# Softmax gradient over 8192 rows: all transfers on one queue, blocks moved as even and odd partitions

## The chip, the cores and the metric

One core of a Trainium2 chip runs the kernel. The metric is the device time of one execution in microseconds (us); lower is better. Before the change it was 1248.48 us, the median of three runs (1247.92 to 1248.65).

A core has engines that run their own instruction streams: TensorE (PE, hardly used here), VectorE (DVE), ScalarE (ACT), GpSimd (POOL) and SyncE (SP, which only issues transfers). Sixteen DMA engines move data between the main memory (HBM) and the on-chip memory (SBUF, 128 partitions). A transfer is issued from an engine's stream: SP and ACT each have a queue of their own, and both queues are served by the same sixteen DMA engines. Engines wait for each other and for transfers by semaphores.

## The reference

The gradient of the cross entropy with respect to the logits: a softmax of every row, less one at the label's place.

```python
logits = np.random.randn(8, 1024, 8192).astype(np.float32)
labels = np.random.randint(0, 8192, (8, 1024)).astype(np.int32)
...
logits_max = np.max(logits, axis=-1, keepdims=True)
exp_logits = np.exp(logits - logits_max)
softmax = exp_logits / np.sum(exp_logits, axis=-1, keepdims=True)
one_hot[batch_idx, seq_idx, labels] = 1.0
return (softmax - one_hot).astype(np.float32)
```

That is 268.4 MB read and 268.4 MB written.

## The kernel before

**Tiling.** The 8192 rows of 8192 floats are cut into B = 32 blocks of 256 rows. Partition p of a block holds the two consecutive rows 2p and 2p+1 (G = 2), each 32 KB, so that a block is 8 MB and, on each partition, 64 KB that lie together in HBM and in SBUF. `X` has room for three blocks (SLOTS = 3); block b lives in slot b % 3, and is worked on in place. What the code calls row t is one of the two rows of every partition, 128 x 8192 floats or 4 MB; there are T = 64 of them, two to a block (t0 and t1).

**The work on one row t.** `row_max` (VectorE) takes the negated maximum of each partition's row. `exponentials` (ACT) writes exp(x - max) over the row, and adds up the sum on the way. `mark` (two ACT instructions) makes one byte for each column, 1 at the label, in a PSUM tile `hot` that has a place for two rows; it may only overwrite a place when `finish` of two rows before is done. `finish` (VectorE) takes the reciprocal of the sum and does exp x reciprocal - byte in one pass over the row. Then the row can be stored.

**Order of the work.** All engines' instructions come from one hand-written loop over blocks. ORDER is "r" for every block: VectorE's stream is max(t1), finish(t0), max(t0 of the next block), finish(t1), and so on. The maximum of the next block's first row is taken, and its exponential issued, before this block is finished, and a row is stored as soon as it is finished.

**Transfers.** Each block's loads and stores have a kind, by the letter in LOADS and STORES, which selects pieces from PIECES: "r" is one row t at a time (128 partitions, runs of 32 KB); "s" is one row as even and as odd partitions (64 partitions, 32 KB); "w" is the whole block (128 partitions, 64 KB). Before, the first three blocks are loaded as "s", the even halves on SP's queue (`nc.sync`) and the odd ones on ACT's (`nc.scalar`); two blocks follow as "r", then 24 as "w" and the last three as "r", all on SP. All stores are "r", on ACT's queue, behind a wait for `finish`. The very last two rows are stored as two halves of columns each (`sides`), the first row on SP and the second on ACT. A load into a slot waits for the stores of the block that was there. `run` adds the waits and the semaphore's increment to an instruction; every instruction of the profile therefore has the line in `run` at which it is issued (L76 before the change).

Of the kernel before, what the change touches and what calls it, by code (L numbers as in the profile page):

```python
# [7 lines left out]
P = 128  # L8
G = 2
SLOTS = 3  # L10

LOADS = "sssrrwwwwwwwwwwwwwwwwwwwwwwwwrrr"
STORES = "rrrrrrrrrrrrrrrrrrrrrrrrrrrrrrrr"
ORDER = "rrrrrrrrrrrrrrrrrrrrrrrrrrrrrrrr"


@with_exitstack
def kernel(
# [6 lines left out]
    nc = tc.nc  # L25
# [11 lines left out]
    T = N // P  # L37
    B = T // G
# [3 lines left out]
    o_b = o_nv.rearrange("(b p j) v -> b p j v", p=P, j=G)  # L42
# [4 lines left out]
    X = const.tile([P, SLOTS, G, V], fp32)  # L47
# [11 lines left out]
    m, s, r = (const.tile([P, T], fp32, name=n) for n in ("m", "s", "r"))  # L59
# [4 lines left out]
    with tc.tile_critical():  # L64
        sem = tc.alloc_semaphore
        got = [[sem(f"got{i}{q}") for q in range(4)] for i in range(SLOTS)]
        put = [[sem(f"put{i}{q}") for q in range(4)] for i in range(SLOTS)]
# [3 lines left out]
        def run(engine, waits, counter, method, **operands):  # L71

            waits = list(dict.fromkeys(waits))
            for w in waits[:-1]:
                engine.wait_ge(*w)  # L75
            instruction = getattr(engine, method)(**operands)  # L76
            for w in waits[-1:]:
                instruction._wait_ge(*w)
            step = 16 if method == "dma_start" else 1
            instruction.then_inc(counter, step)  # L80
            count[counter.name] = count.get(counter.name, 0) + step
            return counter, count[counter.name]

        every, rows = slice(0, P), slice(0, G)
        one = [slice(j, j + 1) for j in range(G)]
        halves = [slice(i, P, 2) for i in range(2)]
        sides = [slice(i * V // 2, (i + 1) * V // 2) for i in range(2)]
        PIECES = {
            "r": [(every, js) for js in one],
            "s": [(ps, js) for js in one for ps in halves],  # L90
            "w": [(every, rows)],
        }

        def meets(a, b):
# [3 lines left out]
        loaded, stored, sides_done = {}, {}, {}  # L98
        maxed, summed, marked, finished, freed = {}, {}, {}, {}, {}

        def load(b):
            loaded[b] = []
            before = stored.get(b - SLOTS, [])
            for q, piece in enumerate(PIECES[LOADS[b]]):
                ps, js = piece
                free = [w for other, w in before if meets(piece, other)]
                queue = nc.scalar if LOADS[b] == "s" and ps == halves[1] else nc.sync
                w = run(
                    queue, free, got[b % SLOTS][q], "dma_start",
                    out=X[ps, b % SLOTS, js, :], in_=x_b[b, ps, js, :],  # L110
                )
                loaded[b].append((piece, w))

        def store(t):
            b, j = divmod(t, G)
            stored.setdefault(b, [])
            if t >= T - G:
                for i, cs in enumerate(sides):
                    w = run(
                        nc.sync if t == T - G else nc.scalar, [sides_done[t][i]], put[b % SLOTS][G * j + i],  # L120
                        "dma_start", out=o_b[b, every, one[j], cs], in_=X[every, b % SLOTS, one[j], cs],
                    )
                    stored[b].append(((every, one[j]), w))
                return
            for q, piece in enumerate(PIECES[STORES[b]]):
                ps, js = piece
                if js.stop != j + 1:
                    continue
                w = run(
                    nc.scalar, [finished[t]], put[b % SLOTS][q], "dma_start",  # L130
                    out=o_b[b, ps, js, :], in_=X[ps, b % SLOTS, js, :],
                )
                stored[b].append((piece, w))

        def row(t):
            return X[:, t // G % SLOTS, t % G, :]
# [4 lines left out]
        def row_max(t):  # L141
            b, j = divmod(t, G)
            arrived = {w[0].name: w for piece, w in loaded[b] if meets(piece, (every, one[j]))}
            maxed[t] = run(
                nc.vector, arrived.values(), dve, "tensor_reduce",
                out=m[:, t : t + 1], in_=row(t), axis=mybir.AxisListType.X, op=Alu.max, negate=True,
            )

        def exponentials(t):
            w = run(  # L150
                nc.scalar, [maxed[t]], act, "activation",
                out=row(t), in_=row(t), func=Act.Exp, bias=m[:, t : t + 1], scale=1.0,
                accum_out=s[:, t : t + 1],
            )
            summed[t] = w

        def mark(t):
            if t >= T:
                return
            w = run(  # L160
                nc.scalar, ([made] if t < G else [freed[t - G]]) + ([marked[t - 1]] if t else []), act, "activation",
                out=away[:], in_=count16[:], func=Act.Abs, bias=at(word, t), scale=1.0,
            )
            marked[t] = run(
                nc.scalar, [w], act, "activation",
                out=hot[:, t % G, :], in_=away[:], func=Act.Relu, bias=at(unit, t), scale=at(minus, t),
            )

        def finish(t):
            w = run(nc.vector, [summed[t]], dve, "reciprocal", out=r[:, t : t + 1], in_=s[:, t : t + 1])  # L170
            bytes_ = hot[:, t % G, :].bitcast(u8)
            sides_done[t] = []
            for i, c in enumerate(sides if t >= T - G else [slice(0, V)]):
                last = run(
                    nc.vector, [marked[t], w] if i == 0 else [], dve, "scalar_tensor_tensor",
                    out=row(t)[:, c], in0=row(t)[:, c], scalar=r[:, t : t + 1], in1=bytes_[:, c],
                    op0=Alu.mult, op1=Alu.subtract,
                )
                sides_done[t].append(last)
            finished[t] = freed[t] = last  # L180

        w_raw = run(nc.scalar, [], lab_got, "dma_start", out=lab_raw[:], in_=lab_bp)
        for b in range(SLOTS):
            load(b)
        w = run(nc.gpsimd, [], pool, "memset", ap=ident[:], constant=0.0)
        w_ident = run(
            nc.gpsimd, [w], pool, "affine_select",
            out=ident[:], in_=ident[:], compare_op=Alu.not_equal, fill=1.0,
# [8 lines left out]
        for j in range(G):  # L197
            w = run(
                nc.tensor, [w_ident, w_lab], pe, "transpose",
                out=lab_ps[:, j, :], in_=lab_f[:, j, :], identity=ident[:],  # L200
            )
        w = run(nc.vector, [w], dve, "tensor_copy", out=lab[:], in_=lab_ps)
        w = run(
            nc.vector, [w], dve, "tensor_scalar",
            out=part[:], in0=lab[:], scalar1=2, scalar2=None, op0=Alu.arith_shift_right,
        )
        w_word = run(
            nc.vector, [w], dve, "tensor_scalar",
            out=word[:], in0=part[:], scalar1=-1.0, scalar2=None, op0=Alu.mult,
        )  # L210
        w = run(
            nc.vector, [w_word], dve, "tensor_scalar",
            out=lab[:], in0=lab[:], scalar1=3, scalar2=None, op0=Alu.bitwise_and,
        )
        w = run(
            nc.vector, [w], dve, "tensor_copy", out=minus[:], in_=lab[:]
        )
# [3 lines left out]
            out=unit[:], in0=minus[:], scalar1=0.0, scalar2=powers[0], op0=Alu.is_equal, op1=Alu.mult,  # L221
# [21 lines left out]
        mark(1)  # L243
        for b in range(B):
            t0, t1 = b * G, b * G + 1
            nxt = t1 + 1
            if ORDER[b] == "b":
                if t0 not in maxed:
                    row_max(t0)
                    exponentials(t0)  # L250
                row_max(t1)
                exponentials(t1)
                finish(t0)
                store(t0)
                mark(t0 + G)
                finish(t1)
                store(t1)
                mark(t1 + G)
                if b + SLOTS < B:
                    load(b + SLOTS)  # L260
                continue
            if t0 not in maxed:
                row_max(t0)
                exponentials(t0)
            row_max(t1)
            finish(t0)
            exponentials(t1)
            store(t0)
            mark(t0 + G)
            ahead = nxt < T and ORDER[b + 1] == "r"  # L270
            if ahead:
                row_max(nxt)
            finish(t1)
            if ahead:
                exponentials(nxt)
            store(t1)
            mark(t1 + G)
            if b + SLOTS < B:
                load(b + SLOTS)
        for b in range(B - SLOTS, B):  # L280
            for _, w in stored[b]:
                nc.scalar.wait_ge(*w)
# [30 lines left out]
```

## Time and profile before

| quantity | value |
|---|---|
| median of three runs | 1248.48 us (1247.92 to 1248.65) |
| span of the profiled execution | 1246.6 us |
| VectorE busy | 1120.2 us (90%), 208 instructions |
| ACT busy | 722.7 us (58%) |
| bytes moved | 536.98 MB, 431 GB/s over the span |
| VectorE waiting for loads | 105.4 us in 26 waits |
| stores, median from issue to landing | 30.4 us for 4 MB |
| loads of whole blocks, median from issue to landing | 33.4 us |

The span goes from the first to the last instruction of one profiled execution; the runs' time has a little around it. The page of the profile cuts the span in 40 slices and gives each engine's busy share in tenths, DMA's too. A group of instructions is given as line, engine, operation, what it writes and reads and in which shapes, then the count, then busy time in us and the mean of one in ns, then the time that the engine stood idle just before them and what ended it. The chain of waits follows the work that ended last, step by step: start, duration, what. "q1" and "q10" are the queues of SP and of ACT. The DMA view of a window lists the packets that start in it: a packet is the run of bytes that one DMA engine moves at a time.

### The profile page before, as it was taken

Reading aid. Unit: us, or ns where it says so; the run is one execution under the profiler, and the core shown is the slowest. Engines: PE = TensorE matmul, PEld = TensorE weight load, DVE = VectorE, ACT = ScalarE, POOL = GpSimd, SP = SyncE. Lnnn points to the kernel's source line nnn. Section 1 sums busy time; section 2 is a strip of 40 time slices with the busy share of each in tenths; the row PEclk is TensorE's granted clock in tenths of the full one; section 3 lists DMA queues with packets and bytes.
Section 4 is the critical chain, followed back from the end, with each engine's and each line's share of the span. In section 5 each row is a group of like instructions: output and inputs, shape, how many; then the busy total and the mean of one; then the engine's idle time right before and its main releaser. Section 6 shows DMA issues by size and latency. Waiting matters only on the chain.

```text
span 1246.6 us, 809 instructions
## 1 busy us (share of the span) xinstructions
PE 0.4 (0%) x2; PEld 0.3 (0%) x2; DVE 1120.2 (90%) x208; ACT 722.7 (58%) x257; POOL 2.3 (0%) x7
## 2 busy tenths in 40 slices
PE   0000000000000000000000000000000000000000
PEld 0000000000000000000000000000000000000000
DVE  5999998889988889888898888998889988899995
ACT  2866664556555565465655655556556555566662
POOL 0000000000000000000000000000000000000000
DMA  9999999999999999999999999999999999999998
GB/s 406 413 431 434 437 432 444 435 437 421 433 429 437 443 423 433 434 431 435 430 441 435 422 435 435 434 440 426 432 434 431 433 446 434 422 430 435 429 434 383
DMA packets 15413, 536.98 MB, mean 431 GB/s; under 512 B 1808, under 2 KB 1808, under 8 KB 1840
## 3 DMA queue, kind: packets, MB, share of 16 engines
q10 hardware_dynamic: 9744, 276.89, 51.5%
q1 hardware_dynamic: 5664, 260.05, 48.3%
q14 instruction: 5, 0.04, 0.0%
HBM read 268.50 MB, written 268.44 MB: 431 GB/s over the span
## 4 chain that ended last, share of the span: by engine, by line
DMA 59%; DVE 26%; issue 11%; ACT 3%; DVEq 0%; ACTq 0%; SPq 0%
DMA X<-in_logits_dram 33%; DMA out_dram<-X 26%; DVE X L76 15%; DVE m L76 10%; ACT X L76 2%; DVEq L64 0%; DVE r L76 0%; ACT hot L76 0%; ACT away L76 0%; ACTq L76 0%; DVEq L75 0%; ACTq L308 0%; SPq L64 0%
## 5 line engine op out<-in xcount | busy, mean ns | idle before, releaser
L76 ACT ACTIVATE X<-X,m 128x8192 f32<-128x8192 f32 x64 | 455.8, 7122 | 365.2 <-DVE m L76 365.2
L76 DVE TENSOR_REDUCE m<-X 128x1 f32<-128x8192 f32 x64 | 555.6, 8682 | 105.4 <-DMA X<-in_logits_dram 105.4
L76 DVE SCALAR_TENSOR_TENSOR X<-X,r,hot 128x8192 f32<-128x8192 f32 (+1 forms) x66 | 560.1, 8489 | 3.8 <-ACT hot L76 1.6
L76 ACT ACTIVATE away<-count,word 128x2048 bf16<-128x2048 int16 x64 | 128.1, 2001 | 127.0 <-DVE X L76 127.0
L76 ACT ACTIVATE hot<-away,unit,minus 128x2048 int32<-128x2048 bf16 x64 | 131.9, 2061 | 2.1
L76 ACT ACTIVATION_READ_ACCUMULATOR X<-X,m 128x1 f32 x64 | 11.9, 186 | 0.0
L76 DVE RECIPROCAL r<-s 128x1 f32<-128x1 f32 x64 | 9.8, 153 | 0.0
L76 ACT ACT_TABLE_LOAD x1 | 1.3, 1283 | 5.3 <-issue 5.3
L76 DVE CAST lab_f<-lab_raw 32x256 f32<-32x256 int32 x1 | 0.5, 536 | 2.7 <-DMA lab_raw<-in_labels_dram 2.7
L76 POOL IOTA count<- 128x2048 int16 x1 | 1.8, 1823 | 0.0
L76 DVE TENSOR_TENSOR unit<-unit,part 128x64 f32<-128x64 f32 x3 | 0.7, 225 | 0.1
L76 DVE CAST lab<-hot 128x64 int32<-128x64 f32 x1 | 0.2, 224 | 0.5 <-PE hot L76 0.5
L76 DVE TENSOR_SCALAR part<-minus 128x64 f32<-128x64 f32 x3 | 0.6, 194 | 0.1
L76 PE MATMUL hot<-ident,lab_f 32*128 32x32 f32 x2 | 0.4, 298 | 3.3 <-DVE lab_f L76 3.3
L76 PEld LDWEIGHTS hot<-ident,lab_f 32*128 32x128 f32 x2 | 0.3, 192 | 3.3 <-DVE lab_f L76 3.3
L76 DVE CAST minus<-lab 128x64 f32<-128x64 int32 x1 | 0.2, 195 | 0.0
L76 DVE TENSOR_SCALAR word<-part 128x64 f32<-128x64 int32 x1 | 0.2, 195 | 0.0
L76 DVE TENSOR_SCALAR lab<-lab 128x64 int32<-128x64 int32 x1 | 0.2, 195 | 0.0
L76 DVE TENSOR_SCALAR unit<-minus 128x64 f32<-128x64 f32 x1 | 0.2, 195 | 0.0
L76 DVE TENSOR_SCALAR part<-lab 128x64 int32<-128x64 int32 x1 | 0.2, 194 | 0.0
L76 DVE TENSOR_SCALAR minus<-unit 128x64 f32<-128x64 f32 x1 | 0.2, 194 | 0.0
L76 POOL TENSOR_SCALAR_AFFINE_SELECT ident<-ident 32x32 f32<-32x32 f32 x1 | 0.2, 203 | 0.1
(5 smaller groups left out, 0.5 us busy)
## 6 DMA issues: line engine op xcount, KB each, us to landing
out_dram<-X ACTq DMA_DIRECT2D x62, 4096.0 KB, 30.4
X<-in_logits_dram SPq DMA_DIRECT2D x10, 4096.0 KB, 28.1
X<-in_logits_dram SPq DMA_DIRECT2D x6, 2048.0 KB, 32.6
X<-in_logits_dram ACTq DMA_DIRECT2D x6, 2048.0 KB, 37.1
out_dram<-X SPq DMA_DIRECT2D x2, 2048.0 KB, 12.7
out_dram<-X ACTq DMA_DIRECT2D x2, 2048.0 KB, 11.9
X<-in_logits_dram SPq DMA_DIRECT2D x24, 33.4
lab_raw<-in_labels_dram ACTq DMA_DIRECT2D x1, 64.0 KB, 1.8
```

The lines of the kernel that those rows point to most:

```text
L76: instruction = getattr(engine, method)(**operands)
```

## The change

Every transfer of the logits and of the output goes to SP's queue; ACT's queue keeps the labels alone. The kinds "s" and "w" are gone. A new kind "q" is a whole block as two transfers, the even partitions (64 of them, 64 KB each) and then the odd ones. The first three loads are "r", all others "q"; the stores of all blocks but the last three are "q", of blocks 29 and 30 "r", and the last block's two rows go out as halves of columns as before, now all four on SP.

`move(b)`, called after both rows of block b are finished, issues in the order TURN: store even, store odd, load even of block b + 3, load odd of block b + 3. A load waits only for the store of the same half. Both stores of a block wait for the `finish` of its second row. The last three blocks are only stored.

The loop's body loses ORDER and with it the work ahead: for each block it is max(t0), max(t1), both exponentials, finish(t0), finish(t1), with each row's `mark` for the next block behind its `finish`. In the new file the issuing line of `run` is L77.

```diff
-LOADS = "sssrrwwwwwwwwwwwwwwwwwwwwwwwwrrr"
-STORES = "rrrrrrrrrrrrrrrrrrrrrrrrrrrrrrrr"
-ORDER = "rrrrrrrrrrrrrrrrrrrrrrrrrrrrrrrr"
+SETS = 2
+TURN = [('S', 0), ('S', 1), ('L', 0), ('L', 1)]
+
+LOADS = "rrrqqqqqqqqqqqqqqqqqqqqqqqqqqqqq"
+STORES = "qqqqqqqqqqqqqqqqqqqqqqqqqqqqqrrr"
...
-        halves = [slice(i, P, 2) for i in range(2)]
+        sets = [slice(i, P, SETS) for i in range(SETS)]
...
             "r": [(every, js) for js in one],
-            "s": [(ps, js) for js in one for ps in halves],
-            "w": [(every, rows)],
+            "q": [(ps, rows) for ps in sets],
...
-        def load(b):
-            loaded[b] = []
+        def load(b, only=None):
+            loaded.setdefault(b, [])
             before = stored.get(b - SLOTS, [])
             for q, piece in enumerate(PIECES[LOADS[b]]):
+                if only is not None and q != only:
+                    continue
                 ps, js = piece
                 free = [w for other, w in before if meets(piece, other)]
-                queue = nc.scalar if LOADS[b] == "s" and ps == halves[1] else nc.sync
                 w = run(
-                    queue, free, got[b % SLOTS][q], "dma_start",
+                    nc.sync, free, got[b % SLOTS][q], "dma_start",
                     out=X[ps, b % SLOTS, js, :], in_=x_b[b, ps, js, :],
                 )
...
-        def store(t):
-            b, j = divmod(t, G)
+        def store(b, only=None):
...
                 w = run(
-                    nc.scalar, [finished[t]], put[b % SLOTS][q], "dma_start",
+                    nc.sync, [finished[b * G + js.stop - 1]], put[b % SLOTS][q], "dma_start",
                     out=o_b[b, ps, js, :], in_=X[ps, b % SLOTS, js, :],
                 )
                 stored[b].append((piece, w))
+
+        def move(b):
+            if b + SLOTS >= B:
+                store(b)
+                return
+            for what, q in TURN:
+                if what == "S":
+                    store(b, q)
+                else:
+                    load(b + SLOTS, q)
...
             row_max(t1)
+            exponentials(t1)
             finish(t0)
-            exponentials(t1)
-            store(t0)
             mark(t0 + G)
-            ahead = nxt < T and ORDER[b + 1] == "r"
-            if ahead:
-                row_max(nxt)
             finish(t1)
-            if ahead:
-                exponentials(nxt)
-            store(t1)
             mark(t1 + G)
-            if b + SLOTS < B:
-                load(b + SLOTS)
+            move(b)
```

More of the change, by code (lines that the diff above doesn't have):

```diff
@@ L112, in load @@
                 loaded[b].append((piece, w))
-        def store(t):
-            b, j = divmod(t, G)
+        def store(b, only=None):
             stored.setdefault(b, [])
[L117 to L123, printed above, removed]
+            if b == B - 1:
+                for t in (T - G, T - 1):
+                    j = t % G
+                    for i, cs in enumerate(sides):
+                        w = run(
+                            nc.sync, [sides_done[t][i]], put[b % SLOTS][G * j + i],
+                            "dma_start", out=o_b[b, every, one[j], cs], in_=X[every, b % SLOTS, one[j], cs],
+                        )
+                        stored[b].append(((every, one[j]), w))
                 return
             for q, piece in enumerate(PIECES[STORES[b]]):
+                if only is not None and q != only:
+                    continue
                 ps, js = piece
-                if js.stop != j + 1:
-                    continue
                 w = run(
-                    nc.scalar, [finished[t]], put[b % SLOTS][q], "dma_start",
+                    nc.sync, [finished[b * G + js.stop - 1]], put[b % SLOTS][q], "dma_start",
                     out=o_b[b, ps, js, :], in_=X[ps, b % SLOTS, js, :],
@@ L245 @@
             t0, t1 = b * G, b * G + 1
[L246 to L251, printed above, removed]
-                exponentials(t1)
-                finish(t0)
-                store(t0)
-                mark(t0 + G)
-                finish(t1)
-                store(t1)
-                mark(t1 + G)
-                if b + SLOTS < B:
-                    load(b + SLOTS)
-                continue
             if t0 not in maxed:
@@ L265 @@
             row_max(t1)
+            exponentials(t1)
             finish(t0)
-            exponentials(t1)
-            store(t0)
             mark(t0 + G)
-            ahead = nxt < T and ORDER[b + 1] == "r"
-            if ahead:
-                row_max(nxt)
             finish(t1)
-            if ahead:
-                exponentials(nxt)
-            store(t1)
             mark(t1 + G)
-            if b + SLOTS < B:
-                load(b + SLOTS)
+            move(b)
         for b in range(B - SLOTS, B):
```

## The prediction

> **What bounds the kernel now.** I read first the head of the page, then the waits of VectorE and the chain of waits, then busy time by stretches, and last the DMA view cut into short windows.
>
> ```profile
> span 1246.6 us, 809 instructions
> PE 0.4 (0%) x2; PEld 0.3 (0%) x2; DVE 1120.2 (90%) x208; ACT 722.7 (58%) x257; POOL 2.3 (0%) x7
> ...
> DMA  9999999999999999999999999999999999999998
> ...
> DMA packets 15413, 536.98 MB, mean 431 GB/s; under 512 B 1808, under 2 KB 1808, under 8 KB 1840
> q10 hardware_dynamic: 9744, 276.89, 51.5%
> q1 hardware_dynamic: 5664, 260.05, 48.3%
> ```
>
> ```profile
> DVE m L76 <- DMA X<-in_logits_dram: 105.4, 26, 8.9
> ```
>
> Two candidates stand close together: VectorE is busy 90% of the span, the DMA engines in every slice. The waits decide: VectorE waits 105.4 us for loads, while the two queues (q10 is ACT's, q1 is SP's) fill 51.5 + 48.3 = 99.8% of the sixteen engines' time. The chain of waits has this form from one block to the next:
>
> ```profile
> 551.04 8.76 DVE X L76
> 559.80 0.02 issue
> 559.82 26.10 DMA out_dram<-X
> 585.92 0.02 issue
> 585.94 33.61 DMA X<-in_logits_dram
> ```
>
> A store lands, frees a slot, a load lands, and only then does VectorE go on. The stretches show how even the flow is:
>
> ```profile
> 0.00:5.00 5.00, 0.41 (x2) 0.28 (x2) 1.58 (x7) 0.00 (x0) 2.31 (x7) 1.00 0.65 223
> 2.00:1243.00 1241.00, 0.41 (x2) 0.28 (x2) 1120.23 (x208) 722.75 (x257) 1.13 (x1) 1.00 1.00 433
> 1240.00:1246.60 6.60, 0.00 (x0) 0.00 (x0) 0.00 (x0) 0.00 (x0) 0.00 (x0) 1.00 0.52 221
> ```
>
> The last two columns are DMA share and GB/s. At 433 GB/s, the first 5 us hold 223 x 5 / 433 = 2.6 us of flow, so flow starts at 2.4 us; the last 6.6 us hold 221 x 6.6 / 433 = 3.4 us, so 3.2 us at the end carry nothing. In between, 1246.6 - 2.4 - 3.2 = 1241.0 us are a full pipe. The kernel is as long as its bytes; a change pays only by making bytes cheaper, and loses by leaving the pipe empty.
>
> **The change, part by part.** *Larger packets.* In the DMA view of the window from 600 to 603 us (queue: packets, MB, share of 16 engines):
>
> ```profile
> q1 hardware_dynamic: 16, 1.05, 80.6%
> q10 hardware_dynamic: 11, 0.36, 27.8%
> ```
>
> The loads' packets are 1.05 MB / 16 = 64 KB and take 0.806 x 16 x 3 us / 16 = 2.418 us each; the stores' are 32 KB and take 0.278 x 48 / 11 = 1.213 us. One large packet saves 2 x 1.213 - 2.418 = 0.008 us against two small ones. Before, 24 loads of 128 partitions have 64 KB runs: 24 x 128 / 16 = 192 packets for each engine. Afterwards it is 29 loaded and 29 stored blocks: 58 x 128 / 16 = 464. So 272 pairs on each engine merge: 272 x 0.008 = 2.2 us. The second way to this price compares the stretch in which loads have 64 KB (160 to 1040 us) with one of 32 KB alone (62 to 160 us):
>
> ```profile
> DMA packets 9787, 381.42 MB, mean 433 GB/s; under 512 B 1072, under 2 KB 1072, under 8 KB 1072
> DMA packets 1469, 42.44 MB, mean 433 GB/s; under 512 B 173, under 2 KB 173, under 8 KB 173
> ```
>
> 381.42 / 880 = 433.4 GB/s against 42.44 / 98 = 433.1, which is 0.09% with half of the bytes in large packets; as 272 x 64 KB x 16 = 285 MB or 53% of all bytes change over, it is 0.09% x 1241 x 0.53 / 0.5 = 1.2 us. I take the middle, **-1.7 us** (bounds -1.2 and -2.2).
>
> *More transfers.* The 1808 packets under 512 B are one for each transfer and engine: 113 transfers. Afterwards there are 131 (one for labels; 6 + 58 loads; 58 + 4 stores and 4 half rows). Their price is bounded in the window from 58.7 to 61.9 us:
>
> ```profile
> q10 hardware_dynamic: 32, 1.05, 105.2%
> q1 hardware_dynamic: 16, 0.00, 0.3%
> ```
>
> Here q1 has only these 16: 0.003 x 3.2 us = 0.01 us for each engine. 18 more cost **+0.2 us** at most.
>
> *Store issues go from ACT to SP, and behind waits.* Issuing costs little:
>
> ```profile
> L76 ACTq DMA_DIRECT2D out_dram<-X x64: 337/338/373, 44.6 to 1233.1; - x64
> L76 SPq DMA_DIRECT2D X<-in_logits_dram x40: 327/328/657, 1.0 to 1173.0; - x40
> ```
>
> 130 issues at about 0.34 us are 44 us of SP's 1246; ACT is relieved of 21 us that it has to spare. But SP works strictly in order, and behind its wait for block b's results stand block b's stores, the loads of b+3 and everything later. Does that wait ever last? The operations of VectorE and ACT:
>
> ```profile
> L76 ACT ACTIVATE X<-X,m 128x8192 f32<-128x8192 f32 x64 | 455.8, 7122 | 365.2 <-DVE m L76 365.2
> L76 DVE TENSOR_REDUCE m<-X 128x1 f32<-128x8192 f32 x64 | 555.6, 8682 | 105.4 <-DMA X<-in_logits_dram 105.4
> L76 DVE SCALAR_TENSOR_TENSOR X<-X,r,hot 128x8192 f32<-128x8192 f32 (+1 forms) x66 | 560.1, 8489 | 3.8 <-ACT hot L76 1.6
> L76 ACT ACTIVATE away<-count,word 128x2048 bf16<-128x2048 int16 x64 | 128.1, 2001 | 127.0 <-DVE X L76 127.0
> L76 ACT ACTIVATE hot<-away,unit,minus 128x2048 int32<-128x2048 bf16 x64 | 131.9, 2061 | 2.1
> L76 DVE RECIPROCAL r<-s 128x1 f32<-128x1 f32 x64 | 9.8, 153 | 0.0
> ```
>
> A block in the new order is two maxima, then two finishes: 2 x (8.68 + 0.15 + 8.76) = 35.2 us of VectorE (8.76 is the full tile in the chain). The first exponential (7.1) lies under the second maximum (8.7), the second under the first finish; the marks (4.1 a row) under the finish and the next maximum. Losing the maximum worked ahead costs nothing while the next block is already in SBUF. One block moves 2 x 8.39 MB / 433 = 38.7 us, so the pipe stays the slower. On the queue, four blocks' worth of half trips (S b+1, L b+4, S b+2, L b+5) lie between a load and the store of the same slot: 77.5 us for 35.2 us of work, 42 us to spare. At the start, row 0 lands near 2.4 + 4.19 / 0.433 = 12.1 us; maximum to 20.8, exponential 28, both pairs of marks 36, second exponential 43.5, second finish about 52.5; the three blocks loaded first occupy the pipe until 2.4 + 58.1 = 60.5. At the end three stores (58 us) outlast the last block's 35. So 0. If the cover were gone, each us late would be paid once and then pushed through the whole queue.
>
> *A load of one half waits for that half's store.* In the DMA view from 585.94 (a load's issue, right when the stores have landed) to 589.55 us, only this queue has packets:
>
> ```profile
> q10 hardware_dynamic: 46, 1.51, 96.6%
> ```
>
> so a load's first packet comes 3.6 us after its issue. Meanwhile the other half of the store, 4.19 MB or 9.7 us, is on the engines. 6 us remain; cost 0.
>
> *One queue instead of two.* From 62.4 to 72.4 us q10 is alone, and the border between two stores lies inside:
>
> ```profile
> DMA packets 150, 4.29 MB, mean 429 GB/s; under 512 B 19, under 2 KB 19, under 8 KB 19
> q10 hardware_dynamic: 150, 4.29, 99.4%
> ```
>
> A single queue keeps the engines at 99.4% over that border (packets are counted where they start, which blurs a 10 us window by about a per cent), so borders in one direction cost nothing. The Trainium skill's DMA: Bandwidth & Descriptors, Anatomy of one DMA, gives each transfer a fixed 2.0 us, mostly the receipt of its last write; charged at each of 122 borders in one queue that would be an estimate of 244 us more, and this row does not bear it out.
>
> *Turns of direction in one queue.* Two queues alternate loads and stores packet by packet at 433 GB/s, so an engine loses nothing when it changes direction with the next packet ready. But the trace has one turn within a queue: ACT's, from the first loads to the first store, the window from 58.7 to 61.9 us above. The 32 packets of 32 KB took 1.052 x 16 x 3.2 / 32 = 1.683 us, 0.47 too long, twice on each engine: 0.94 us. It was also the first store of all, with all engines starting together, as the first loads do (window from 2.3 to 4.1 us):
>
> ```profile
> q1 hardware_dynamic: 16, 0.52, 100.6%
> ```
>
> 1.006 x 1.8 = 1.811 us, 0.60 over 1.213, and not repeated later. Loads that resume against running stores (589.55 to 591.0 us) show little:
>
> ```profile
> q1 hardware_dynamic: 16, 1.05, 171.9%
> ```
>
> 1.719 x 1.45 = 2.493 us, 0.075 over 2.418. The new order makes 29 more turns of each kind, so a turn into stores lies between 0 and 0.94 us, one into loads between 0 and 0.60. I take 0 for both, by the alternation, which happens some thousand times, against single events at a cold start.
>
> *Sum:* -1.7 + 0.2 = -1.5 us; span 1245.1. The runs' median, 1248.48, is 1.9 us above the profiled 1246.6, so **1247.0 us**.
>
> **The rivals.** *Slower, turns cost.* Place: each passage of SP's queue from a block's loads to the next stores. It decides beyond the band from (2.5 + 1.5) / 29 = 0.14 us a turn. At the full 0.94 it gives 1247.0 + 27.3 = 1274.3; with one slow packet of the two, 0.47, it gives **1260.6**. For it: the only such turn on record is slow. Against: it was the first store. With 0.60 for the way back too, 1292.
>
> *Slower, every border drains.* If a queue alone restarts cold at each of 122 new borders, 122 x 0.60 = 73 us: **1320**. The 99.4% speak against it. (A fixed cost for each transfer, as the Trainium skill's DMA: Bandwidth & Descriptors, Anatomy of one DMA, has it, would show in this form.)
>
> *Faster.* The 24 resumed loads' 0.075 us come from two queues meeting; with one they vanish: 24 x 0.075 = 1.8 us more, **1245.2**. Against: that a load begins late need not come from the other queue.
>
> *The change does nothing.* If packets of both sizes share one true rate, 433 GB/s, the time is **1248.7** (0.2 more transfers).
>
> **How the numbers follow.** Within 0.2% (2.5 us, 1246.0 to 1251.0) is what a measurement of this kernel can't tell from no change. Forecast 0.44, of it 0.08 below 1246.0; turns cost 0.33, of it 0.02 within the band; borders 0.04; faster 0.12; nothing 0.07. Faster 0.08 + 0.12 = 0.20; same 0.36 + 0.02 + 0.07 = 0.45; slower 0.31 + 0.04 = 0.35. The forecast's own range is 1245.0 to 1249.5. To leave out no more than 2 in 10, the range goes to 1244.0 below (0.04 left) and into the turns up to 1268.0, 0.73 us a turn (0.10 of that case left, and 0.04 of the borders).
>
> **What the profile would show.** Right: one large queue at about 99.8% of the engines, few packets of 32 KB, 433 to 434 GB/s in all slices, SP's stores never waiting for VectorE in mid-kernel, VectorE waiting for loads some 3 us a block. Packets of the first store after a load longer than 2.418 us, or slices below 430 GB/s throughout, would show the turns. VectorE without waits, and the DMA with holes, would mean that working by block sets the pace; stores issued long after the queue has emptied, that the order of waits does. A time over 1251 or under 1246 makes the forecast wrong.

## The result, and the profile after

| | before | after |
|---|---|---|
| median | 1248.71 us (1247.92 to 1249.81, 10 runs) | 1251.46 us (1249.64 to 1254.61, 10 runs) |
| ratio | | 1.0023, 95% interval 1.0014 to 1.0031 |
| span of the profiled execution | 1246.6 us | 1248.9 us |

The change makes the kernel slower, by 0.23%, and its runs differ more from each other: 5.0 us between fastest and slowest against 1.9 us. 1251.46 us lies inside the stated range of 1244.0 to 1268.0, but the forecast was a gain of 1.5 us, and the prediction's last line has a time over 1251 against it.

The head of the page after the change, and VectorE's longest wait for transfers:

```profile
span 1248.9 us, 855 instructions
PE 0.4 (0%) x2; PEld 0.3 (0%) x2; DVE 1120.1 (90%) x208; ACT 722.7 (58%) x257; POOL 2.3 (0%) x7
...
DMA packets 11351, 537.00 MB, mean 430 GB/s; under 512 B 2096, under 2 KB 2096, under 8 KB 2128
q1 hardware_dynamic: 11296, 536.88, 99.6%
```

```profile
DVE m L77 <- DMA X<-in_logits_dram: 92.3, 25, 4.5
```

All bytes are on one queue, which keeps the sixteen DMA engines busy 99.6% of the span; a quarter of the packets is gone (11351 for 15413); VectorE does the same work and waits less, 3.7 us a block. So the order of work and the waits on SP's queue are as foreseen. The loss must be in how the bytes move. Busy time by stretches, with DMA share and GB/s last:

```profile
0.00:5.00 5.00, 0.00 (x0) 0.00 (x0) 0.31 (x1) 1.28 (x1) 2.31 (x7) 1.00 0.64 223
2.00:1243.00 1241.00, 0.42 (x2) 0.29 (x2) 1120.09 (x208) 722.75 (x257) 1.13 (x1) 1.00 1.00 432
1240.00:1248.90 8.90, 0.00 (x0) 0.00 (x0) 0.00 (x0) 0.00 (x0) 0.00 (x0) 1.00 0.40 171
```

By the prediction's reckoning, flow starts at 5 - 223 x 5 / 433 = 2.4 us as before. The last 8.9 us hold 171 x 8.9 / 433 = 3.5 us of flow, so 5.4 us at the end are empty, where it was 3.2. The part between is 1248.9 - 2.4 - 5.4 = 1241.1 us, against 1241.0. So the middle gained nothing, and 2.2 us were lost at the end.

The end can be seen. This is the DMA share in tenths from 1240 to 1249 us, in slices of 0.225 us, after the change:

```profile
DMA  9369689683663653813531131010010000000000
```

and before it:

```profile
DMA  9969869699396583100100000000000000000000
```

Before, the engines finish close together: the last sixteen packets under 512 B in the trace start between 1242.5 and 1244.9 us. Afterwards the engines drop out one by one, and these packets start between 1242.0 and 1247.3 us. Each engine has the same number of packets, so some have fallen behind on the way. Each transfer ends with a packet under 512 B on each of the sixteen engines, and the DMA view of a window that just holds the sixteen of one transfer tells how far apart the engines are. After the change, from 12.3 to 12.9 us and from 1174.0 to 1179.1 us:

```profile
DMA packets 32, 0.52 MB, mean 874 GB/s; under 512 B 16, under 2 KB 16, under 8 KB 16
DMA packets 56, 2.62 MB, mean 514 GB/s; under 512 B 16, under 2 KB 16, under 8 KB 16
```

Before the change, from 1203.6 to 1206.3 us on ACT's queue:

```profile
DMA packets 55, 1.28 MB, mean 473 GB/s; under 512 B 16, under 2 KB 16, under 8 KB 16
```

In 0.6 us at the start, in 5.1 us late in the changed kernel, in 2.7 us late in the old one. Where the time went is visible at the turns, where the direction changes between loads and stores. The first turn, at 56 to 61 us, costs 0.85 us on the mean of the engines, much as in the kernel before (0.94), so it makes no difference. The window from 97.5 to 100.5 us holds the first store packets after the loads of block 3, one for each engine:

```profile
q1 hardware_dynamic: 16, 1.05, 82.4%
```

0.824 x 3 = 2.472 us each, 0.054 over 2.418. Later turns cost up to about 0.25 us on the mean of the engines, unequally, and fade after 620 us.

Call what a packet takes over the usual 2.418 us (64 KB) or 1.213 us (32 KB) a stall. Summed over the packets of the trace and the sixteen engines, the stalls are 63 us after the change (55 before 620 us, 8 later) and 42 us before it (32 and 10). That is 21 / 16 = 1.3 us more on the mean of the engines, about what the larger packets were to give. The 2.2 us come on top, because the kernel ends with the slowest engine.

### The profile page after: what moved, and what is told of

Read it like the earlier page. It is cut to its first block, busy times and chain, and to the rows that moved or that the text cites. A ratio compares the mean times of both kernels' runs of the same rounds, so it can differ in the third digit from the quotient of the medians.

```text
span 1248.9 us, 855 instructions
## 1 busy us (share of the span) xinstructions
PE 0.4 (0%) x2; PEld 0.3 (0%) x2; DVE 1120.1 (90%) x208; ACT 722.7 (58%) x257; POOL 2.3 (0%) x7
## 2 busy tenths in 40 slices
DMA packets 11351, 537.00 MB, mean 430 GB/s; under 512 B 2096, under 2 KB 2096, under 8 KB 2128
## 3 DMA queue, kind: packets, MB, share of 16 engines
q1 hardware_dynamic: 11296, 536.88, 99.6%
## 4 chain that ended last, share of the span: by engine, by line
DMA 84%; DVE 8%; SPq 2%; issue 2%; ACT 2%
DMA out_dram<-X 81%; DVE X L77 5%; DVE m L77 4%; DMA X<-in_logits_dram 3%; SPq L77 2%; ACT X L77 1%; ACT hot L77 0%; ACT away L77 0%; DVE r L77 0%; SPq L296 0%; SPq L65 0%
## 5 line engine op out<-in xcount | busy, mean ns | idle before, releaser
L77 DVE TENSOR_REDUCE m<-X 128x1 f32<-128x8192 f32 x64 | 553.0, 8680 | 92.3 <-DMA X<-in_logits_dram 92.3
L77 ACT ACTIVATE X<-X,m 128x8192 f32<-128x8192 f32 x64 | 455.8, 7122 | 286.3 <-DVE m L77 286.3
L77 DVE SCALAR_TENSOR_TENSOR X<-X,r,hot 128x8192 f32<-128x8192 f32 (+1 forms) x66 | 560.1, 8489 | 3.9 <-ACT hot L77 1.6
L77 ACT ACTIVATE away<-count,word 128x2048 bf16<-128x2048 int16 x64 | 128.1, 2001 | 199.1 <-DVE X L77 148.1
L77 ACT ACTIVATE hot<-away,unit,minus 128x2048 int32<-128x2048 bf16 x64 | 131.9, 2062 | 2.1
L77 DVE RECIPROCAL r<-s 128x1 f32<-128x1 f32 x64 | 9.9, 155 | 2.4 <-ACT X L77 2.4
L77 ACT ACTIVATION_READ_ACCUMULATOR X<-X,m 128x1 f32 x64 | 11.9, 186 | 0.0
L77 DVE CAST lab_f<-lab_raw 32x256 f32<-32x256 int32 x1 | 0.4, 373 | 4.7 <-DMA lab_raw<-in_labels_dram 4.7
L77 POOL IOTA count<- 128x2048 int16 x1 | 1.8, 1824 | 0.0
L77 DVE TENSOR_TENSOR unit<-unit,part 128x64 f32<-128x64 f32 x3 | 0.7, 224 | 0.1
L77 DVE CAST lab<-hot 128x64 int32<-128x64 f32 x1 | 0.2, 224 | 0.5 <-PE hot L77 0.5
L77 DVE TENSOR_SCALAR part<-minus 128x64 f32<-128x64 f32 x3 | 0.6, 195 | 0.1
L77 PE MATMUL hot<-ident,lab_f 32*128 32x32 f32 x2 | 0.4, 302 | 5.1 <-DVE lab_f L77 5.1
L77 PEld LDWEIGHTS hot<-ident,lab_f 32*128 32x128 f32 x2 | 0.3, 196 | 5.1 <-DVE lab_f L77 5.1
L77 DVE TENSOR_SCALAR part<-lab 128x64 int32<-128x64 int32 x1 | 0.2, 196 | 0.0
L77 DVE TENSOR_SCALAR word<-part 128x64 f32<-128x64 int32 x1 | 0.2, 195 | 0.0
L77 DVE TENSOR_SCALAR minus<-unit 128x64 f32<-128x64 f32 x1 | 0.2, 195 | 0.0
L77 DVE TENSOR_SCALAR lab<-lab 128x64 int32<-128x64 int32 x1 | 0.2, 195 | 0.0
L77 DVE CAST minus<-lab 128x64 f32<-128x64 int32 x1 | 0.2, 195 | 0.0
L77 DVE TENSOR_SCALAR unit<-minus 128x64 f32<-128x64 f32 x1 | 0.2, 195 | 0.0
L77 POOL TENSOR_SCALAR_AFFINE_SELECT ident<-ident 32x32 f32<-32x32 f32 x1 | 0.2, 203 | 0.1
```

## The experiments

Theory T: in one queue all DMA engines turn from loads to stores together, some of them stall there, and each turn costs about the same. Theory S, formed from T after the first four runs: the stalls pull the engines apart until they no longer meet. The other theories blame the halves (C, and H2 in two queues), the work by block (O) or the stores' 64 KB runs in two queues (H).

### Stores back on ACT's queue

```diff
-                    nc.sync, [finished[b * G + js.stop - 1]], put[b % SLOTS][q], "dma_start",
+                    nc.scalar, [finished[b * G + js.stop - 1]], put[b % SLOTS][q], "dma_start",
```

> The changed kernel with its stores (but the last block's four half rows) issued from ACT's queue again; cut, sizes and order of work stay. Theory T (in one queue all DMA engines turn from loads to stores together, once a block, and some of them stall there, which also pulls the engines apart): with two queues loads and stores overlap, the stalls every 38.7 us vanish, and what is left is the larger packets' gain: about 1247.5 us, 1246.5 to 1248.7. Rival C (the cut into even and odd partitions makes the DMA engines uneven, in whatever queue): 1251, as the changed kernel. Rival O (working by block costs the time): 1251 too.

Measured: 1259.32 us (1256.98 to 1267.14), ratio 1.0101 (1.0080 to 1.0122). No theory had it. The stalls sum to 101 us here, 34 of them at 91 to 95 us, where the first halves are loaded against stores, and late in the kernel the sixteen ends of one store lie 11 us apart (1091.5 to 1102.7 us). So two queues do not by themselves keep the engines together. The last experiment returns to this.

### Rows instead of halves, one queue

```diff
-LOADS = "rrrqqqqqqqqqqqqqqqqqqqqqqqqqqqqq"
-STORES = "qqqqqqqqqqqqqqqqqqqqqqqqqqqqqrrr"
+LOADS = "r" * 32
+STORES = "r" * 32
```

> The changed kernel with every load and store one row of 128 partitions in 32 KB runs, on SP's queue alone in the same order (two stores, two loads). Theory T: the turns stay, the larger packets' gain of about 1 us is lost: 1252.5 us, 1251.5 to 1254. Rival C (even and odd partitions): the cut is gone, so 1248.5 to 1249.5. Rival O (work by block): 1252.

Measured: 1253.38 us (1252.68 to 1253.69), ratio 1.0041 (1.0029 to 1.0053). As T expected: the loss is there without any halves, and 1253.38 - 1251.46 = 1.9 us (2.2 by the ratios to the kernel before) is what the larger packets are worth in one queue. Between these two kernels 464 pairs of packets merge on each engine, 3.7 us at 0.008 us each, so only about half of the saving reaches the end of the kernel. The engines stand even further apart than in the changed kernel; the sixteen ends of one transfer need the window from 1176.0 to 1182.1 us:

```profile
DMA packets 98, 2.69 MB, mean 440 GB/s; under 512 B 16, under 2 KB 16, under 8 KB 16
```

The trace does not name the engine of a packet, but in one queue a packet starts where the last one of its engine ended, so most engines can be followed. Fifteen of the sixteen can be in this run: ten have stalls of 2.1 to 3.1 us in all and end between 1244.0 and 1244.6 us, five have 5.1 to 8.2 us and end between 1246.9 and 1249.9. The late engines are those that stalled more.

### Work by block in the kernel before

```diff
-ORDER = "rrrrrrrrrrrrrrrrrrrrrrrrrrrrrrrr"
+ORDER = "b" * 32
```

> The kernel before with its order of work set to one block at a time; all transfers as before. Theory T and rival C: VectorE's order is hidden by the transfers, 1248.7 us within 0.7. Rival O: about 1251.

Measured: 1248.41 us (1247.74 to 1249.53), ratio 1.0002 (0.9993 to 1.0011). The order of VectorE's work is free here; rival O is out. Against the run with rows in one queue, this one has two queues and loads in 64 KB runs for 24 blocks. At 0.008 us for each of the 192 merged pairs of an engine these are worth 1.5 us, so of the 1253.38 - 1248.41 = 5.0 us between the two about 3.5 go with the single queue. (With it, a row is also stored only when its whole block is finished; the two were not tried apart.)

### Twice the turns

```diff
-            for what, q in TURN:
-                if what == "S":
-                    store(b, q)
-                else:
-                    load(b + SLOTS, q)
+            store(b, 0)
+            if b:
+                load(b + SLOTS - 1, 1)
+            store(b, 1)
+            load(b + SLOTS, 0)
```

(The odd half of the last load is issued ahead of block 29's stores.)

> The changed kernel with the order on SP's queue store even of b, load odd of b+2, store odd of b, load even of b+3: loads and stores alternate by 4 MB, so the direction turns twice as often, and each load has two other transfers before it as cover. Theory T: twice the stalls, about 2 to 4 us more than the changed kernel: 1253.5 to 1255.5 us. Rivals C and O: 1251.5, as the changed kernel. Less than 1250 would mean that it is the long stretches in one direction, not the turns, that cost.

Measured: 1251.87 us (1250.57 to 1252.79), ratio 1.0028 (1.0018 to 1.0038), the same as the changed kernel's. T in its first form falls: the cost does not go by the number of turns. That made theory S.

### Whole blocks, two queues

In the kernel with stores on ACT:

```diff
-SETS = 2
-TURN = [('S', 0), ('S', 1), ('L', 0), ('L', 1)]
+SETS = 1
+TURN = [('S', 0), ('L', 0)]
```

> Stores on ACT's queue, loads on SP's, every block whole: one transfer of 128 partitions in 64 KB runs each way; work by block as in the changed kernel. All packets are as large as in the changed kernel, without halves and without turns in one queue. Theory S (in one queue all DMA engines turn together, meet, and are pushed apart until they no longer meet; mixed traffic of two queues leaves them together and unharmed): the larger packets' gain of about 1 us shows, 1247.5 us, 1246.5 to 1248.4. Rival H (in two queues it is the stores in 64 KB runs that bring the loss of the run with stores on ACT, not the halves): 1255 or more.

Measured: 1286.44 us (1285.54 to 1295.63), ratio 1.0318 (1.0296 to 1.0341). Far from S's 1247.5. The chain of waits of this run (start, duration, what) shows one possible bound, the round trip of a slot:

```profile
527.67 16.00 DVE m L77 x2
...
553.91 8.76 DVE X L77
...
564.79 41.54 DMA out_dram<-X
606.33 0.02 issue
606.34 41.62 DMA X<-in_logits_dram
647.97 0.02 issue
647.99 16.00 DVE m L77 x2
```

From one pair of maxima to the next of the same slot it is 647.99 - 527.67 = 120.3 us: 41.6 to load, 37.1 to work, 41.5 to store. Three slots share this, 40.1 us a block, more than the 38.7 that the bytes need. Two queues share the engines, so a load and a store that overlap take twice as long each. But the round trip is not the whole loss. The two queues of this run:

```profile
q1 hardware_dynamic: 5616, 276.83, 51.7%
q10 hardware_dynamic: 4800, 260.11, 47.0%
```

51.7 + 47.0 = 98.7% of 1283.8 us are 1267.1 us of packets on each engine, where the changed kernel has 99.6% of 1248.9, 1243.9 us, for the same bytes. So 23 of the 35 us between the two are longer packets, and at most 12 an idle pipe. Without longer packets a load with a store beside it would take 38.7 us at 433 GB/s, and a round trip about (38.7 + 37.1 + 38.7) / 3 = 38.2 us a block, an estimate, and less than the bytes need. So S is wrong in that two queues leave the engines unharmed, at least with whole blocks, and H is not ruled out: both directions have 64 KB runs here.

### Whole blocks, one queue

The same edit in the changed kernel.

> The changed kernel with each block as one transfer of 128 partitions instead of two halves, all on SP's queue: store b, then load b+3, which waits for it with nothing queued behind the store. All theories agree that the queue runs empty once a block: by 0.35 us from the last byte to the release and 1.4 to 3.6 us from the issue to the first packet, 29 times, 50 to 115 us more than the changed kernel: 1300 to 1365 us. Below 1260 would mean that the halves are not needed as cover.

Measured: 1357.1 us (1356.88 to 1357.31), ratio 1.0869 (1.0850 to 1.0888), 105.6 us over the changed kernel. The halves are needed as cover. One period goes from one load's issue to the next, 634.59 to 677.03 us, 42.4 us. The DMA view of one whole period, from 635 to 677.44 us, with both ends in an empty stretch:

```profile
DMA packets 288, 16.78 MB, mean 395 GB/s; under 512 B 32, under 2 KB 32, under 8 KB 32
q1 hardware_dynamic: 288, 16.78, 95.7%
```

4.3% of a period, 1.8 us, is an empty queue. And the 288 - 32 = 256 large packets took 0.957 x 16 x 42.44 / 256 = 2.538 us each, 0.120 over 2.418; at 16 for each engine and block that is 1.9 us a block. So about half of the 105.6 us is the empty queue, and the other half is stalls. The DMA engines start each block's load together here, and pay at every block what the changed kernel pays rarely: the first packets of the load at 636 us are 0.68 us too long on the mean of the engines, those of the store behind it, at 653 us, 1.24 us.

The empty stretch has two parts. The last packet of the store ends at 634.22 us and the load is issued at 634.59, 0.37 us later; the load's first packet starts at 635.55, 0.96 us after its issue. (The rest of the 1.8 us is that some engines end earlier and some start later.) The Trainium skill's DMA: Bandwidth & Descriptors, Anatomy of one DMA, has about 2.0 us fixed for a transfer, mostly the receipt of its last write; that section describes transfers issued from GpSimd, and these are issued from SP. The trace is near in the size, 1.8 us, but not in the division: 0.37 us lie before the next issue and 0.96 behind it. The Trainium skill's DMA: Bandwidth & Descriptors, Rules for kernel authors, advises one transfer of 128 partitions over two halves, since both use the same engines. Here the two halves were the faster way, by 105.6 us, about half of it because the second one runs while the landing of the first is waited for.

### Halved stores, two queues

In the kernel of whole blocks in two queues:

```diff
-TURN = [('S', 0), ('L', 0)]
+TURN = [('S', 0), ('S', 1), ('L', 0)]
...
+            "w": [(every, rows)],
```

(SETS is 2 again, and LOADS is "w" from the fourth block on.)

> As e5_whole_two_queues, but the stores go as even and odd partitions (loads stay whole, 128 partitions). Theory H2 (halves of 64 partitions in two queues at once are what cost 10 us with stores on ACT): 1254 to 1262 us. Rival (it was the halved loads, each released by its own half): 1247.5 us as e5_whole_two_queues.

Measured: 1342.84 us (1335.34 to 1347.55), ratio 1.0749 (1.0719 to 1.0780). Worse than either theory. VectorE waits far longer for loads than the whole stores let it:

```profile
L77 DVE TENSOR_REDUCE m<-X 128x1 f32<-128x8192 f32 x64 | 553.0, 8680 | 194.6 <-DMA X<-in_logits_dram 194.6
```

194.6 us, against 137.9 in the run of whole blocks. Here too most of the loss is longer packets:

```profile
q1 hardware_dynamic: 5616, 276.83, 51.8%
q10 hardware_dynamic: 5264, 260.12, 46.5%
```

98.3% of 1338.6 us are 1315.8 us of packets on each engine, 72 more than in the changed kernel. That halved stores in two queues cost extra beyond whole ones (1267.1 us) fits H2. Why the packets are longer is not shown.

### Drained once

```diff
+            if b == 14:
+                for _, w in loaded[b + SLOTS - 1]:
+                    nc.sync.wait_ge(*w)
             for what, q in TURN:
```

> The changed kernel with one wait more: before block 14's stores, SP waits for the loads of block 16 to land, so the queue runs empty once and all DMA engines start together again at about 600 us. The empty queue itself costs 2 to 4 us. Theory S (stalls end once the engines stand apart): the stalls, 55 of 64 us (summed over 16 engines) before 620 us in the changed kernel and 8 after, come again after the new start: over 20 us in the second half, the spread of the engines grows from under 1 us to 3 or more once more; 1254.5 to 1259 us in all. Rival T (each turn costs about the same, and the quiet second half was chance): second half about 8 us or no pattern, 1253.5 to 1255.5 us.

Measured: 1258.34 us (1256.92 to 1259.03), ratio 1.0077 (1.0064 to 1.0090): 6.9 us for one drain. Here S can be watched. Sixteen ends of a transfer before the drain (593.5 to 598.3 us), after it (659.5 to 660.3) and late (1181.9 to 1187.8):

```profile
DMA packets 47, 2.03 MB, mean 423 GB/s; under 512 B 16, under 2 KB 16, under 8 KB 16
...
DMA packets 32, 1.05 MB, mean 1311 GB/s; under 512 B 16, under 2 KB 16, under 8 KB 16
...
DMA packets 63, 3.08 MB, mean 522 GB/s; under 512 B 16, under 2 KB 16, under 8 KB 16
```

4.8 us, 0.8 us, 5.9 us: the drain puts the engines back in step, and they move apart again. The first packets at the next two turns, into loads (626 to 629 us) and into stores (646 to 649 us):

```profile
q1 hardware_dynamic: 16, 1.05, 104.4%
...
q1 hardware_dynamic: 16, 1.05, 116.7%
```

1.044 x 3 = 3.13 us and 1.167 x 3 = 3.50 us, that is 0.71 and 1.08 us over 2.418 on the mean of the engines, with the queue full and long after the first store. Summed as before, the stalls are 43 us before 620 us and 50 us after, 31 of these at the two turns just shown, where the changed kernel had 55 and 8. S expected over 20 in the second half; T about 8.

### A gentle start, two queues

In the kernel with stores on ACT:

```diff
-LOADS = "rrrqqqqqqqqqqqqqqqqqqqqqqqqqqqqq"
-STORES = "qqqqqqqqqqqqqqqqqqqqqqqqqqqqqrrr"
+LOADS = "rrrrrrqqqqqqqqqqqqqqqqqqqqqqqrrr"
+STORES = "rrrqqqqqqqqqqqqqqqqqqqqqqqrrrrrr"
```

> The kernel of e1_stores_on_act (stores on ACT, halves) with rows of 128 partitions for the first six loaded and the first three stored blocks, and for the last three loaded and the last six stored, halves of 64 KB between. In e1 the DMA engines moved 433 to 434 GB/s in most slices, but one fell 11 us behind, after a burst of 34 us of stalls at 91 us (first halves loaded against stores) and others after 970 us. Theory S: without that start the engines stay within 3 us of each other and the larger packets show: 1247 to 1249 us. Rival (halves in two queues drive the engines apart at any time): 1254 or more.

Measured: 1457.99 us (1441.05 to 1476.78), ratio 1.1614 (1.1567 to 1.1661). The rival was right, and far too mild. In the window from 300 to 420 us this kernel and the one with stores on ACT run the same loop, halves of 64 KB in two queues. The DMA view of this one (of an execution of 1470.11 us):

```profile
DMA packets 799, 41.62 MB, mean 347 GB/s; under 512 B 164, under 2 KB 164, under 8 KB 164
q1 hardware_dynamic: 398, 20.78, 49.1%
q10 hardware_dynamic: 401, 20.84, 44.7%
```

and of the one with stores on ACT:

```profile
DMA packets 1004, 52.36 MB, mean 436 GB/s; under 512 B 205, under 2 KB 205, under 8 KB 205
q1 hardware_dynamic: 497, 26.28, 50.6%
q10 hardware_dynamic: 507, 26.08, 50.2%
```

The loads' 20.78 MB are 317 packets of 64 KB, which take 0.491 x 16 x 120 / 317 = 2.97 us each, against 26.28 MB, 401 packets and 2.42 us. The engines are also idle for 6% of the window here. The two kernels differ only in the kinds of their first and last blocks, and the same loop in the middle runs at 436 or at 347 GB/s. Halves in two queues are not safe, and the 1259.32 of the first experiment looks like a favourable arrangement of them; what makes one favourable was not tried. No version tried beats the kernel before.

## Why the prediction was wrong

- **What bounds the kernel** was right: the bytes. VectorE's 1120.1 us stayed hidden.
- **Larger packets, -1.7 us**, was right in kind, but less of it reaches the end of the kernel: the packets take 2.418 us for 2 x 1.213 as foreseen, but the 1.9 us (or 2.2) between rows and halves in one queue are for 464 merged pairs, so 1.1 to 1.3 us for the 272 of the change, about the lower bound of 1.2. That bound was itself weakly based: 0.09% between two windows is no more than the blur that the prediction names, a per cent in 10 us and so 0.1% in 98 us. **More transfers, +0.2**, held: 18 more packets under 512 B on each engine, of 0.009 us in the trace, are 0.16 us.
- **Order of work and the waits on SP, 0**, held. The kernel before with work by block takes 1248.41 us. The second finish ended at 53.4 us, for 52.5 reckoned.
- **A load waits for its half's store, 0**, held. The price without the cover (whole blocks) was 105.6 us, within the 50 to 115 reckoned for an empty queue before that run, but partly by luck: only about half of it is the empty queue, 1.8 us a block, and the rest is stalls, which were not in that sum.
- **One queue instead of two** was right for borders in one direction, but it was put on the wrong footing for the rest: a single queue does cost, about 3.5 us by the runs with rows, where stores also start later.
- **Turns of direction, 0**, is the step that failed. The prediction named the mechanism as its first rival, with the right row, the packets from 58.7 to 61.9 us that were 0.94 us too long on each engine, and then took 0, since two queues alternate directions without loss, and since that turn was the first store of all. The drained kernel shows the same price, 1.08 us, at a turn in mid-kernel, so it was no matter of the first store. What it did not have is that the price is not the same each time: after a common start one or two turns are dear, and those that follow cost a few hundredths to a quarter of a us, as the engines stand apart. In the changed kernel the dear turn is the first, which the kernel before pays as well; it is the later, unequal stalls that cost.
- **The price**, as the last engine sees it: the span was to shrink by 1.5 us and grew by 2.3, together 3.8 us or 0.13 us a turn, just about where the rival was said to decide (0.14). Of these, 1.3 us are more stalls on the mean of the engines and 2.2 us the greater distance of the last one; 0.3 us are left over. The rival's 1260.6 was three times too much.
- **The end** was not in the sum at all. The prediction took the 3.2 empty us at the end as given. They hold the distance between the first and the last engine, and grew to 5.4.

What stays open: why the engines stall when they turn together. The distance between them is not the whole condition either: at 97.5 us the engines of the changed kernel still stood close, and the turn cost 0.054 us, where the drained kernel's cost 1.08. That the unequal ends are the sum of unequal stalls is read from the traces (the ten and five engines of the run with rows), and was not tried by itself. No run took the turns out of a single queue and got the time back: the one that put the stores back on a second queue stalled more, elsewhere.

## What to carry to other kernels

- A kernel bound by DMA ends when the slowest DMA engine ends. Look at how far the engines stand apart at the end of a transfer, and at how the share falls off in the last us; the mean rate hides both.
- One queue with halves gives each transfer the full rate and covers the landing of the half before, which matters when the buffers' round trip is short. But it turns all engines at once. With two queues and stores by rows, as in the kernel before, they stayed closer together (2.7 us for 5.1), and the kernel was 0.23% faster. Two queues alone do not do it: with halves in both the engines drifted 11 us apart, and the kernel was slower.
- A row that shows an event only once prices it at a cold start; it does not say that the event is cheap later.

## What the runs showed of the hardware

- Packets of 64 KB in halves of 64 partitions, loads on one queue and stores on the other, ran at 436 or 347 GB/s in the same loop of two kernels that differ in their first and last blocks (windows from 300 to 420 us above).
- The sixteen engines, with equal bytes, drift 5.1 us apart over 1.2 ms in the changed kernel's one queue, 2.7 us in the two queues of the kernel before, and 11 us with halves in two queues. A drain takes them back to 0.8 us, at a price of 6.9 us in all, more than the empty queue (1.8 us a time in the kernel of whole blocks).
- From the last packet of an 8 MB store to the issue of the load that waits for it the trace shows 0.37 us, and from there to the load's first packet 0.96 us, in an otherwise empty queue (whole blocks in one queue).
